# An encoder layer's two branch projections by seven block products, with lasting buffer pools and a pinned order around the feed-forward and the end

## The chip, the cores and the metric

One NeuronCore of a Trainium2 chip. The metric is the device time of one execution in microseconds (us), the median over several.

## The reference, cut to what matters

One layer is applied to two groups of 512 tokens (g = 0, 1) with the same weights; the model width is 1024, so a tensor is 8 column blocks of 128.

```python
h = rmsnorm(x, g_mix); u = h @ w_in            # split into q, k, v, o, gates, c_q, c_kv, ..., gm
y_m = (sigmoid(o) * hm) @ w_mo                 # hm: normalised mLSTM output
y_a = mla_attention(...) @ w_ao                # 8 heads
g_m, g_a = split(sigmoid(gm))
x = x + (g_m * y_m + g_a * y_a) @ w_out
h2 = rmsnorm(x, g_ffn)
x = x + (silu(h2 @ w_gate) * (h2 @ w_up)) @ w_down      # width 2816 = 22 blocks
x = x + sigmoid(x @ w_ple_gate) * (p @ w_ple)
return rmsnorm(x, g_final)
```

All data is float32. The kernel gets its precision from split operands: a tensor is a high part (rounded, on ScalarE) and a low part (the rest, one subtraction on VectorE), and a product is three matmuls: high x high, low x high, high x low.

## The kernel before, in words

Tokens lie along the free dimension (tiles of 128 x 512, 256 KB); a weight block is 128 x 1024 (512 KB) and is loaded, split and used as the stationary operand. A list scheduler that works with a model of the engines' times sets the order on each engine from the data dependencies, the free buffers and the program's order as priority; a few places are tied by hand (`issue_after`). All DMAs are issued by SP, in one queue. Buffers come from pools (`Slots`) that are opened and closed like a stack; a new pool's tile waits until the tiles that lay on its memory have been read.

The order of the program:

- The input projection's parts, the mLSTM by head, then attention by head (`attn_proj`, `attn`, L668-L738). The merge gates' projections (`merge_gate`, list `BULK`) lie between the heads; their results go to DRAM (`tmd`, `tad`), as do the branches' results (`hzd`, `ozd`).
- Projection of the mLSTM branch, L761-L771: `hx` is split (`gsplit`), then per column block c `w_mo` and both groups, 24 matmuls each by `proj1` (L152-L163). The PSUM pool is attention's (tag `mm`), and the operands take buffers that attention's latents leave, so these products may run between attention's. Results go to DRAM (`z1d`).
- Projection of the attention branch, L772-L791: the same with `w_ao`; merge; split into `y`.
- Output projection, L800-L812: per block c `w_out` for both groups, residual, squares for the norm (`SumSq`).
- The norms of both groups (L813, `rstd_bank`, `spread`: root on VectorE, two diagonal tiles, two matmuls that spread it over the partitions), and the embedding product `p @ w_ple`, 16 blocks of 6 matmuls, tied behind the last output projection (L817-L822). Then pools O, H, EV and WP are closed and OP is opened on their memory (L824-L831).
- Feed-forward operands, L931-L947: per k four normalised tiles, split, and four sums of them on POOL for the seven products.
- Feed-forward by `Seven` (L838-L908): a quad is two weight blocks times both groups with the inner dimension halved, a 2 x 2 by 2 x 2 block product, done by seven products P1, P2, P7, P6, P5, Q4, P3 of 4 x 3 = 12 matmuls (9 in the last part of down) that accumulate in PSUM banks b0, b1, b2. It needs sums of weight blocks (POOL, L879-L889) and of operands. The first gate quad is computed plainly with 96 matmuls (`plain`, L855-L869), while the operands come into being. `run` (L910-L920) chains quads, with the next quad's P1, P2, P7 between the present one's P6, P5, Q4, P3; it is called once for gate and up and once per part of down (three parts, L1037), whose operands are loaded back from DRAM (`actd`) and split first.
- The end, L1040-L1133: `x` is split again, `proj2` multiplies by `w_ple_gate`, `embed` applies tanh, the embedding and the residual, `final_norm` (L1077-L1096) scales and writes. Group 0 is done four blocks ahead of group 1; the last two blocks of group 1 go by token halves.

## Time and profile before

| | |
|---|---|
| median of 3 executions | 1949.64 us (1948.28 to 1950.61) |
| the profiled execution's own time | 1949.27 us |
| its span, first to last instruction | 1947.5 us |
| busy: PE / DVE / ACT / POOL | 95% / 59% / 43% / 21% |
| mean granted TensorE clock | 0.978 |

Times in the profile's rows are us from the span's start. PE is TensorE's matmuls, PEld its weight loads, DVE is VectorE, ACT is ScalarE, POOL is GpSimd, SP issues DMAs. A row names the line of the kernel before, the engine, the operation and `out<-in` by the program's tile names. Matmuls overlap each other, so their busy time is longer than the distance from one to the next.

### The profile page before, as it was taken

The numbers are of one execution on the slowest core, as the hardware profiler recorded it, in microseconds if no ns is written. First come the engines' busy times: TensorE is split into PE (matmuls) and PEld (weight loads), VectorE is DVE, ScalarE is ACT, GpSimd is POOL, SyncE is SP. The second block draws the span as 40 slices with busy tenths as digits, with TensorE's granted clock in tenths as the row PEclk, the third lists the DMA queues.
The fourth block names the chain that finished last, engine by engine and source line by source line (L and its number), as shares of the span: only waits on it lengthen the run. The fifth ranks groups of instructions, "written<-read, shape, count | busy, mean of one in ns | idle before, by whom it ended". The sixth has DMA issues, their size and how long they took to land.

```text
span 1947.5 us, 24431 instructions
## 1 busy us (share of the span) xinstructions
PE 1855.9 (95%) x8922; PEld 1554.3 (80%) x8922; DVE 1146.6 (59%) x2021; ACT 830.9 (43%) x1608; POOL 400.5 (21%) x313
## 2 busy tenths in 40 slices
PE   7999999999999999999999948999999989999993
PEld 6889898988888788788888827888888867888883
DVE  7757575746455666854445455444454448967655
ACT  5245454535354566852122234333333335533332
POOL 3000000100000000100001033665566472323002
PEclk9999999999999999999999978999999999999996
DMA  4111111012252212457335110232232337633322
GB/s 160 50 44 33 55 44 55 33 60 82 82 181 87 71 63 82 136 194 227 109 112 191 64 65 27 95 127 92 98 115 102 103 127 246 197 100 99 108 65 87
DMA packets 94424, 198.15 MB, mean 102 GB/s; under 512 B 10272, under 2 KB 20896, under 8 KB 94304
## 3 DMA queue, kind: packets, MB, share of 16 engines
q1 hardware_dynamic: 94304, 196.59, 30.0%
q8 instruction: 70, 1.15, 0.2%
q14 instruction: 50, 0.41, 0.1%
HBM read 142.45 MB, written 54.10 MB: 101 GB/s over the span
## 4 chain that ended last, share of the span: by engine, by line
PE 88%; DVE 6%; ACT 2%; DMA 1%; issue 1%; POOL 1%; SPq 0%; DVEq 0%; ACTq 0%; POOLq 0%
PE mm L160 11%; PE mm L162 11%; PE mm L161 11%; PE b L904 10%; PE b L905 10%; PE b L906 10%; PE nm L548 3%; DVE xl L133 2%; PE mm L465 2%; PE mm L467 2%; PE mm L466 2%; PE mm L1065 1%; PE mm L1066 1%; PE mm L1064 1%; PE pt L726 1%
## 5 line engine op out<-in xcount | busy, mean ns | idle before, releaser
L904 PE MATMUL b<-xh,wh 128*128 128x512 f32 x896 | 346.0, 391 | 13.7 <-ACT xh L137 7.7
L905 PE MATMUL b<-xl,wh 128*128 128x512 f32 x896 | 349.6, 390 | 0.0
L906 PE MATMUL b<-xh,wl 128*128 128x512 f32 x896 | 346.5, 390 | 0.0
L133 DVE TENSOR_TENSOR wl<-wst,wh 128x512 fp32r<-128x512 f32 (+1 forms) x226 | 200.9, 890 | 154.9 <-ACT wh L851 134.0
L851 ACT CAST wh<-wst 128x512 fp32r<-128x512 f32 (+1 forms) x202 | 122.7, 609 | 284.2 <-PE b L905 246.4
L160 PE MATMUL mm<-hh,whi 128*128 128x512 f32 x592 | 233.4, 395 | 7.2 <-ACT whi L147 7.0
L162 PE MATMUL mm<-hh,wlo 128*128 128x512 f32 x592 | 232.6, 395 | 2.3 <-DVE wlo L133 2.2
L161 PE MATMUL mm<-hl,whi 128*128 128x512 f32 x592 | 233.5, 395 | 0.8 <-DVE hl L247 0.8
L904 PEld LDWEIGHTS b<-xh,wh 128*128 128x128 f32 x896 | 168.9, 189 | 50.9 <-ACT xh L137 8.2
L906 PEld LDWEIGHTS b<-xh,wl 128*128 128x128 f32 x896 | 168.9, 188 | 35.3
L905 PEld LDWEIGHTS b<-xl,wh 128*128 128x128 f32 x896 | 168.9, 188 | 35.2 <-DVE xl L133 0.2
L147 ACT CAST whi<-wst 128x1024 fp32r<-128x1024 f32 (+1 forms) x79 | 81.5, 1032 | 142.9 <-PE mm L161 122.6
L160 PEld LDWEIGHTS mm<-hh,whi 128*128 128x128 f32 x592 | 112.5, 190 | 30.8 <-ACT whi L147 7.0
L162 PEld LDWEIGHTS mm<-hh,wlo 128*128 128x128 f32 x592 | 112.4, 190 | 26.2 <-DVE wlo L133 3.4
L161 PEld LDWEIGHTS mm<-hl,whi 128*128 128x128 f32 x592 | 112.2, 189 | 25.2 <-DVE hl L247 1.9
L879 POOL TENSOR_TENSOR s<-wst,wst 128x512 f32<-128x512 f32 (+1 forms) x33 | 44.9, 1359 | 386.4 <-DMA wst<-w 300.4
L133 DVE TENSOR_TENSOR wlo<-wst,whi 128x1024 fp32r<-128x1024 f32 (+1 forms) x79 | 96.5, 1221 | 28.3 <-ACT whi L147 27.6
L133 POOL TENSOR_TENSOR vnl<-avt,vnh 128x512 fp32r<-128x512 f32 x16 | 21.1, 1317 | 357.8 <-ACT vnh L137 217.1
L962 DVE TENSOR_TENSOR u<-b,u 128x512 f32<-128x512 f32 x63 | 43.4, 688 | 71.1 <-PE b L906 71.1
L1014 DVE TENSOR_TENSOR x<-x,b 128x512 f32<-128x512 f32 x84 | 56.9, 681 | 38.1 <-PE b L906 37.9
L465 PE MATMUL mm<-whi,hh 128*128 128x256 f32 x256 | 72.0, 283 | 0.4 <-DVE cu L299 0.4
L466 PE MATMUL mm<-whi,hl 128*128 128x256 f32 x256 | 72.0, 283 | 0.0
(311 smaller groups left out, 3977.4 us busy)
## 6 DMA issues: line engine op xcount, KB each, us to landing
wst<-w SPq DMA_DIRECT2D x125, 512.0 KB
ld<-actd SPq DMA_DIRECT2D x77, 256.0 KB
actd<-t SPq DMA_DIRECT2D x44, 256.0 KB
actd<-sg SPq DMA_DIRECT2D x33, 256.0 KB
x<-x SPq DMA_DIRECT2D x32, 256.0 KB
wst<-wd SPq DMA_DIRECT2D x16, 512.0 KB
hzd<-hz SPq DMA_DIRECT2D x16, 256.0 KB
tmd<-tg SPq DMA_DIRECT2D x16, 256.0 KB
```

What stands on the lines that cost most here:

```text
L133: e.tensor_tensor(out=out, in0=src, in1=hi.bitcast(F32), op=ALU.subtract)
L147: S.copy(hi[:, :n], st[:, :n])
L160: E.matmul(bk, whi[:, c], hi, start=k == 0, stop=False)
L161: E.matmul(bk, whi[:, c], lo, start=False, stop=False)
L162: last_mm[0] = E.matmul(bk, wlo[:, c], hi, start=False, stop=k == nk - 1)
L465: E.matmul(out, hi[:, tb], whi[:, n], start=k == 0, stop=False)
L466: E.matmul(out, lo[:, tb], whi[:, n], start=False, stop=False)
L548: E.matmul(bk, l, r, start=n == 0, stop=n == len(terms) - 1)
L851: S.copy(hi, src)
L904: E.matmul(bk, whi[:, c], hi, start=bool(first) and k == 0, stop=False, **sk)
L905: E.matmul(bk, whi[:, c], lo, start=False, stop=False, **sk)
L906: E.matmul(bk, wlo[:, c], hi, start=False, stop=k == self.kh - 1, **sk)
```

## The change

- `w_mo` and `w_ao`: blocks c and c+4 of a weight form a quad for `Seven`; the eight quads run in one chain (`chain`, in place of `run`), which calls for operands (`need`) four products ahead. The class `Ops` makes a product's operand when it is called for; sums of operands are on VectorE or POOL by a rule of each use. Three of the mLSTM branch's operands are called for before attention's last head. The chain's PSUM banks are opened behind attention.
- Pools H, EV, WP, a new WX and the new OP last to the end; split weights take turns in five buffers of WP and WX. The X2 pool, which later holds `x`, holds the raw operands.
- The output projection does all blocks of group 0 and then all of group 1, so that each `w_out` block is loaded and split twice. Group 0's norm lies inside group 1's products (`mid`).
- The root is spread by four matmuls of its column, broadcast, with the identity (`spread_f32`), in place of two diagonal tiles and two matmuls.
- From the last output projection on the order on PE, ACT, DVE and POOL is the program's (`pinned`); the embedding products are dealt out between the steps of group 1's norm and the first operands.
- All feed-forward quads, gate/up and down, form one chain; the first gate quad goes by seven products too; the chain begins with P1 and P2 of two quads.
- In the end group 0 is six blocks ahead, the order is pinned, group 0's output lies between group 1's blocks, and the token halves of the last two blocks are interleaved.

The diff, cut to its core:

```diff
--- before.py
+++ after.py
+    pinned = [False]
+
+    class Engine:
+
+
+        def __init__(self, e):
+            self.e = e
+
+        def __getattr__(self, name):
+            f = getattr(self.e, name)
+
+            def call(*args, **kw):
+                r = f(*args, **kw)
+                if pinned[0]:
+                    tc.keep_in_program_order(r)
...
-    def proj1(w, x, nk=KD, off=0, bn="mm", tok=slice(0, T)):
+    def proj1(w, x, nk=KD, off=0, bn="mm", tok=slice(0, T), mid=None):
         whi, wlo = w
         bk = bank(bn)[:, tok]
         for k in range(nk):
             c = slice(off + k * P, off + (k + 1) * P)
+            if mid and k == nk - 3:
+                mid()
...
+    def spread_f32(r, b0=0, nb=NB, bn="rbc"):
+        bc = bank(bn)
+        for i in range(nb):
+            E.matmul(
+                bc[:, (b0 + i) * P : (b0 + i + 1) * P], r[:, 2 * i : 2 * i + 1].to_broadcast([P, P]), ident,
+                start=True, stop=True,
+            )
+        return bc[:, b0 * P : (b0 + nb) * P]
...
+    Q = Slots("Q", tr=3, qkv=12, qst=4, p=3, ph=1, pl=1)
     QL = Slots("QL", lat=16)
-    Q = Slots("Q", tr=3, qkv=12, qst=4, p=3, ph=1, pl=1)
...
+    WX = Slots("WX", "right", wst=2, s3=2, wp=1)
...
-        w = w8(f"mo{c}")
-        for g in range(G):
-            t = load(tmd[g][c], QL, "lat")
-            V.scalar_tensor_tensor(out=t, in0=t, scalar=1.0, in1=proj1(w, hx[g]), op0=ALU.add, op1=ALU.mult)
-            nc.sync.dma_start(z1d[g][c], t)
...
-    OP = Slots("OP", op=OPS, ev=8)
...
+    def op(name, n, dt):
+        return (H if name in ("P1", "P2", "P7", "P6") else late["OP"])("h", n, dt)
...
+        def part(self, name, k):
+            if name in ("P1", "P2", "P3"):
+                return self.get({"P1": "a", "P2": "c", "P3": "d"}[name], k)
+            add = self.sums(name).tensor_tensor
+            if name == "P7":
+                t = self.t[k] = self.tmp()
+                add(out=t, in0=self.get("b", k), in1=self.get("d", k), op=ALU.subtract)
+            elif name == "P6":
+                t = self.t[k]
+                add(out=t, in0=t, in1=self.get("a", k), op=ALU.subtract)
+            elif name == "P5":
+                t = self.get("a", k)
+                add(out=t, in0=t, in1=self.get("b", k), op=ALU.subtract)
+            else:
+                t = self.t[k]
+                add(out=t, in0=t, in1=self.get("c", k), op=ALU.add)
+            return t
...
+        sl, tag = ((WP, "whi"), (WP, "wlo"), (WX, "wp"), (WP, "whi"), (WP, "wlo"))[wpn[0] % 5]
+        wpn[0] += 1
+        return sl(tag, "wp", F32R, (P, 1024))
...
-        def plain(self, put):
-
-            ws = [[self.split(self.st[2 * i + j]) for j in range(2)] for i in range(2)]
...
+    def chain(quads, head=False, look=4):
+
+        order = [(0, n) for n in ("P1", "P2", "P7")]
...
+            order = [(0, "P1"), (0, "P2"), (1, "P1"), (1, "P2"), (0, "P7"), (0, "P6"), (0, "P5"), (0, "Q4"), (1, "P7"), (0, "P3")]
...
+            for i, m in order[at : at + look + 1]:
+                quads[i][0].need(m)
+            for i, m in order[at : at + 2]:
+                if i not in made:
+                    made[i] = quads[i][1]()
+            made[q].product(n)
...
+            QL.close()
+            X2 = Slots("X2", "right", x=16)
+            for n in ("P1", "P2", "P7"):
+                hops.need(n)
...
+    late["OP"] = Slots("OP", h=24, sg=4, ev=8)
...
+    banks("PF", dict(b0=2, b1=3, b2=2, sp=1), b0="b0", b1="b1", b2="b2", sp="sp")
...
+            m = load4(tmd[g][cc])
+            V.scalar_tensor_tensor(out=m, in0=m, scalar=1.0, in1=t, op0=ALU.add, op1=ALU.mult)
+            nc.sync.dma_start(z1d[g][cc], m)
...
+            z = load4(z1d[g][cc])
+            y = load(tad[g][cc], late["OP"] if c == 0 else X2, "sg" if c == 0 else "x")
+            V.scalar_tensor_tensor(out=y, in0=y, scalar=1.0, in1=t, op0=ALU.add, op1=ALU.mult)
+            V.tensor_tensor(out=y, in0=y, in1=z, op=ALU.add)
+            yr[g][cc] = y
...
+    oops = Ops(lambda g, k: load(ozd[g][k], X2, "x"), lambda: late["OP"]("ev", "t"), lambda n: V if n == "P7" else GP)
...
+    chain([pair("mo", c, hops, put_z(c)) for c in range(4)] + [pair("ao", c, oops, put_y(c)) for c in range(4)])
...
+        for k in (0, 4, 1, 5, 2, 6, 3, 7):
+            t = yr[g][k]
+            hi = H("h", "yh", F32R)
+            S.activation(out=hi, in_=t, func=AF.Copy, scale=0.5)
+            lo = H("h", "yl", F32R)
+            V.scalar_tensor_tensor(out=lo, in0=t, scalar=0.5, in1=hi.bitcast(F32), op0=ALU.mult, op1=ALU.subtract)
+            y[g][k] = (hi, lo)
...
+    h2 = Ops(hn, lambda: OP("ev", "t"), lambda n: GP if n == "Q4" else V)
...
+    for c in range(KD):
+        out_proj(0, c)
+    pp, wple = [], []
+    for c in range(KD):
+        pinned[0] = c == KD - 1
+        out_proj(1, c, {0: lambda: sums(0), 1: lambda: spread2(0)}.get(c))
+        if c == 0:
+            inv(0)
+        if 2 <= c < 6:
+            h2.need("P1", [c - 2])
+            h2.need("P2", [c - 2])
...
+    emb(2)
+    sums(1)
+    emb(1)
+    inv(1)
+    emb(1)
+    spread2(1)
+    emb(2)
+    for k in range(4):
+        h2.get("b", k)
+        h2.get("d", k)
+        emb(1)
+        h2.need("P7", [k])
+        emb(1)
+    emb(len(todo))
+    pinned[0] = False
+    for n in ("P6", "P3", "P5", "Q4"):
+        h2.need(n)
...
-        if f1 == 0:
-            make("fg", None)().plain(gate)
-            return [make("fu", up)]
...
+    chain(quads, head=True)
...
+    for c in range(LEAD):
+        w = halves(c)
         for g in range(G):
             embed(c, g, proj2(w, x3[g]))
-    for c in range(lead, KD):
-        embed(c, 0, proj2(wpg(c), x3[0]))
-    ws = [wpg(c) for c in range(lead, lead + 2)]
-    final_norm(0)
-    for c in range(lead, KD - 2):
-        bk = proj2(ws.pop(0), x3[1])
-        ws.append(wpg(c + 2))
-        embed(c, 1, bk)
-    last = [load(emd[1][c], OP, "ev") for c in range(KD - 2, KD)]
-    for b0, nb in ((0, NB // 2), (NB // 2, NB // 2)):
-        tok = slice(b0 * P, (b0 + nb) * P)
-        for c in range(KD - 2, KD):
-            embed(c, 1, proj2(ws[c - KD + 2], x3[1], tok), tok, last[c - KD + 2])
-        final_norm(1, b0, nb, (2, 5) if b0 else range(KD))
+    for c in range(LEAD, KD):
+        embed(c, 0, proj2(halves(c), x3[0]))
+    w = halves(LEAD)
+    pinned[0] = True
...
+    bk = [proj2(ws[0], x3[1], toks[0])]
+    embed(*last)
+    finish(0, [4, 5])
+    bk.append(proj2(ws[1], x3[1], toks[0]))
+    embed(KD - 2, 1, bk[0], toks[0], bps[0])
+    finish(0, [6])
+    bk.append(proj2(ws[0], x3[1], toks[1]))
+    embed(KD - 1, 1, bk[1], toks[0], bps[1])
+    finish(0, [7])
+    sums(1, 0, H0)
+    inv(1, H0)
+    bk.append(proj2(ws[1], x3[1], toks[1]))
+    embed(KD - 2, 1, bk[2], toks[1], bps[0])
+    spread3(1, 0, H0)
+    finish(1, [0, 1, 2, 3], 0, H0)
+    embed(KD - 1, 1, bk[3], toks[1], bps[1])
+    sums(1, H0, H0)
+    inv(1, H0)
+    rs_ = rs2[1]
+    spread3(1, H0, H0)
+    rs2[1], rs_ = rs_, rs2[1]
+    finish(1, [4, 5, 6, 7], 0, H0)
+    rs2[1] = rs_
+    finish(1, list(range(KD)), H0, H0)
```

## Rows read from the trace of the kernel before

**Rows 1.** The page: busy time by engine, and PE's share in 40 slices, in tenths.

```profile
PE 1855.9 (95%) x8922; PEld 1554.3 (80%) x8922; DVE 1146.6 (59%) x2021; ACT 830.9 (43%) x1608; POOL 400.5 (21%) x313
...
PE   7999999999999999999999948999999989999993
```

**Rows 2.** One line's instructions, L160: ns min/median/max, first and last start us.

```profile
L160 PE MATMUL mm<-oxh,whi x128: 389/389/389, 936.1 to 1022.5; 128*128 128x512 f32 x128
...
L160 PE MATMUL mm<-yh,whi x128: 389/389/389, 1023.2 to 1109.5; 128*128 128x512 f32 x128
```

**Rows 3.** Stages: length, busy us (instructions) of each engine, granted clock, DMA share, GB/s.

```profile
817.00:872.00 55.00, 55.00 (x269) 45.70 (x268) 37.31 (x78) 38.05 (x73) 2.97 (x2) 1.00 0.64 216
936.00:1023.00 87.00, 87.00 (x386) 72.03 (x385) 40.30 (x54) 17.91 (x23) 0.00 (x0) 1.00 0.33 107
1109.50:1196.30 86.80, 52.59 (x216) 40.66 (x215) 53.97 (x81) 32.95 (x56) 25.75 (x17) 0.78 0.13 49
1130.00:1175.00 45.00, 10.79 (x33) 6.21 (x31) 30.52 (x33) 14.72 (x26) 18.15 (x12) 0.62 0.09 33
1200.00:1580.00 380.00, 380.00 (x1678) 314.64 (x1677) 175.59 (x209) 137.10 (x237) 224.58 (x150) 1.00 0.31 105
1580.00:1627.00 47.00, 35.31 (x147) 27.96 (x145) 28.22 (x42) 23.32 (x41) 17.20 (x13) 0.93 0.60 206
1627.00:1700.00 73.00, 71.87 (x308) 59.00 (x309) 63.26 (x90) 37.20 (x64) 22.50 (x15) 0.98 0.58 195
1700.00:1815.00 115.00, 115.00 (x509) 95.20 (x509) 84.08 (x126) 41.92 (x75) 33.44 (x25) 1.00 0.33 106
```

**Rows 4.** PE's waits: for whom; us in total, times, longest.

```profile
PE b L866 <- ACT xh L137: 33.2, 4, 12.4
```

**Rows 5.** Timeline, ScalarE, then VectorE: start, us, [idle before, releaser].

```profile
1135.14 0.59 ACT L821 COPY em<-mm 128x512 f32<-128x512 f32 x1 [0.77 <-PE mm L162]
1135.63 0.62 ACT L137 CAST xh<-hn 128x512 fp32r<-128x512 f32 x1
...
1136.28 0.69 DVE L133 TENSOR_TENSOR xl<-hn,xh 128x512 fp32r<-128x512 f32 x1 [13.98 <-ACT xh L137]
1136.89 0.74 DVE L935 SCALAR_TENSOR_TENSOR hn<-x,cols,rbc 128x512 f32<-128x512 f32 x1
```

**Rows 6.** Timeline, PE, first products of the plain gate quad.

```profile
1176.21 0.63 PE L866 MATMUL b<-xh,wh 128*128 128x512 f32 x1
1176.64 0.63 PE L867 MATMUL b<-xl,wh 128*128 128x512 f32 x1
```

**Rows 7.** Timeline, PE, where gate/up gives way to down.

```profile
1605.52 1.22 PE L904 MATMUL b<-xh,wh 128*128 128x512 f32 x2 [7.74 <-ACT xh L137]
```

**Rows 8.** Timeline of the end: PE, VectorE, ScalarE, PE.

```profile
1913.01 0.28 PE L1066 MATMUL mm<-xh,wl 128*128 128x256 f32 x1
...
1907.11 6.20 DVE L1092 SCALAR_TENSOR_TENSOR o<-x,cols,rsf 128x512 f32<-128x512 f32 x6 [4.12 <-ACT rsf L1081]
...
1927.28 3.30 ACT L1089 ACTIVATE o<-x,cols 128x256 f32<-128x256 f32 x8
1930.48 0.36 ACT L1107 ACTIVATE pt<-mm 128x256 f32<-128x256 f32 x1
...
1935.76 0.98 PE L198 MATMUL ssc<-onesr,sq 128*128 128x2 f32 x4 [8.78 <-DVE sq L236]
```

**Rows 9.** Stages, instructions on tile mm alone (w_mo's products beside attention).

```profile
817.00:845.00 28.00, 12.16 (x44) 8.12 (x44) 0.00 (x0) 0.00 (x0) 1.00 0.91 308
845.00:872.00 27.00, 16.82 (x70) 12.93 (x71) 2.64 (x4) 0.00 (x0) 1.00 0.36 120
```

**Rows 10.** Groups by line and form: feed-forward (VectorE, POOL), projections 936-1110 (VectorE): busy, mean ns.

```profile
L133 DVE TENSOR_TENSOR wl<-wst,wh 128x512 fp32r<-128x512 f32 x120 | 118.4, 987 | 123.5 <-ACT wh L851 123.5
...
L879 POOL TENSOR_TENSOR s<-wst,wst 128x512 f32<-128x512 f32 x20 | 26.0, 1300 | 101.8 <-DMA wst<-w 101.6
...
L133 DVE TENSOR_TENSOR pll<-ld,plh 128x512 fp32r<-128x512 f32 x4 | 2.7, 690 | 3.5 <-ACT plh L137 3.5
```

More of the change, by code (lines that the diff above doesn't have):

```diff
@@ L833, in split_op, with __init__, get, need @@
-    def split_op(src):
-        return split(src, OP, "op", "x")
+    late = {}
+    NAMES = ("P1", "P2", "P7", "P6", "P5", "Q4", "P3")
+    def op(name, n, dt):
+        return (H if name in ("P1", "P2", "P7", "P6") else late["OP"])("h", n, dt)
+    class Ops:
+        def __init__(self, raw, tmp, sums):
+            self.raw, self.tmp, self.sums = raw, tmp, sums
+            self.r, self.t, self.x = {}, {}, {}
+        def get(self, n, k):
+            if (n, k) not in self.r:
+                self.r[n, k] = self.raw({"a": 0, "b": 1, "c": 0, "d": 1}[n], k + 4 * (n in "cd"))
+            return self.r[n, k]
+        def part(self, name, k):
[15 more added lines that the diff above has]
+            return t
+        def need(self, name, ks=range(4)):
+            x = self.x.setdefault(name, [])
+            for k in ks:
+                if len(x) == k:
+                    src = self.part(name, k)
+                    hi = op(name, "xh", F32R)
+                    S.copy(hi, src)
+                    lo = op(name, "xl", F32R)
+                    lo_of(lo, src, hi)
+                    x.append((hi, lo))
@@ new lines, in encoder_kernel, with __call__, sums, inv @@
+    OP = late["OP"]
+    banks("P3", dict(mm=5, tp=1, bc=2), mm="mm", tp="ssc", bc="rbc")
+    class Sl:
+        def __call__(self, tag, n, dt=F32, shape=(P, T)):
+            return OP("ev" if tag in ("ch", "tr") else "h", n, dt, shape)
+    sl = Sl()
+    x2 = [[None] * KD for _ in range(G)]
+    ss = [SumSq(sl, "tr") for _ in range(G)]
+    pc, r2, rs2 = {}, {}, {}
+    def sums(g, b0=0, nb=NB):
+        pc[g] = bank("ssc")
+        sumsq(pc[g], ss[g].sq, b0, nb)
+    def inv(g, nb=NB):
+        r2[g] = rsqrt(pc[g][:, 0 : 2 * nb], 2 * nb, 1.0 / D)
@@ L1038, in encoder_kernel @@
     f0 = 0
     for pi, nf in enumerate(FF_PARTS):
-        run(down(pi, f0, nf))
+        quads += down(pi, f0, nf // 2)
         f0 += nf
+    chain(quads, head=True)
     banks("P4", dict(mm=5, tp=1, bc=2), mm="mm", tp="ssc", bc="rbc")
-    def halves(src):
-        st = W("wst", "wst", F32, (P, 1024))
-        nc.sync.dma_start(st, src)
-        out = []
-        for j in range(2):
-            hi = W("wh", "wh", F32R)
-            S.copy(hi, st[:, j * T : (j + 1) * T])
-            lo = W("wl", "wl", F32R)
-            lo_of(lo, st[:, j * T : (j + 1) * T], hi)
-            out.append((hi, lo))
-        return out
@@ L1058, in proj2, with halves @@
-    def proj2(ws, x, tok=slice(0, T)):
+    x3 = [[None] * KD for _ in range(G)]
+    for c in range(KD):
+        for g in range(G):
+            x3[g][c] = split(x2[g][c], H, "h", "x")
+    ss = [SumSq(sl, "h") for _ in range(G)]
+    def halves(c):
+        st = (WP, WX)[c % 2]("wst", "wst", F32, (P, 1024))
+        nc.sync.dma_start(st, a["w8"][W8[f"pg{c}"]])
+        return [wsplit(st[:, j * T : (j + 1) * T]) for j in range(2)]
+    def proj2(ws, x, tok=slice(0, T), mid=None):
         bk = bank()[:, tok]
@@ new lines, in encoder_kernel @@
+    ws = [w, halves(KD - 1)]
+    bps = [load(emd[1][c], OP, "ev") for c in range(KD - 2, KD)]
+    toks = [slice(0, T // 2), slice(T // 2, T)]
+    H0 = NB // 2
+    bk = [proj2(ws[0], x3[1], toks[0])]
+    embed(*last)
+    finish(0, [4, 5])
[7 more added lines that the diff above has]
+    inv(1, H0)
```

386 lines of the change are left out of this document (185 added, 201 removed).

## The prediction

> **What bounds the kernel now.** I read the page first. TensorE (PE) is busy 95% of the span and no other engine over 59%; the 40 slices show 9 nearly everywhere, with dips at slices 24-25, at slice 33 and in the last one [rows 1]. So only two things can shorten this kernel: fewer matmul columns, or less time in which PE stands. The price of a matmul is not its 389 ns of busy time, since matmuls overlap: the w_ao projection's 384 matmuls start at 936.1 and w_out's at 1023.2 [rows 2], so one costs 87.1/384 = 0.227 us, and a block product of 12 costs 2.72 us. Then the table by stage [rows 3] gives the holes: 936-1023, 1200-1580 and 1700-1815 are full, 1130-1175 has 10.8 busy of 45.0, 1580-1627 has 35.3 of 47.0, and the end stands largely empty (part 4 below). The waits [rows 4] say who ends the first hole: ScalarE's split of the feed-forward operands, 33.2 us in 4 waits. ScalarE in turn begins those splits at 1135.6, right behind its last copy of the embedding product, although the first normalised operand had been written long before [rows 5]: the operands' pool lies on the memory of the pools that the embedding product still uses. From there VectorE builds operands in a row: 0.74 for one normalised tile, 0.69 for one low part [rows 5].
>
> **1. Seven products instead of eight.** For w_mo and w_ao two column blocks c and c+4 and both groups took 4 x 24 = 96 matmuls; the seven products take 7 x 12 = 84. Eight such quads save 96 matmuls, the first gate quad of the feed-forward (plain before) another 12. 108 x 0.227 = **24.5 us** off, all on PE, which is full there [rows 3].
>
> **2. In front of the feed-forward.** From the last w_out matmul (1109.5) to the first regular product (1196.3) are 86.8 us [rows 3]. Work that stays in it: 96 embedding matmuls and 96 of the plain quad, 192 x 0.227 = 43.5. The other **43.3 us** are holes, and matmuls at the lower of the two clocks (1.2 GHz): granted 0.62 of 2.4 GHz on average in 1130-1175, with 0.43 us between two matmuls still at 1176 [rows 3, 6]. The change makes the pools last, so that operands need not wait for the embedding product; projects group 0 through w_out before group 1 (43.6 us of matmuls under which group 0's norm and eight of its splits fit); and pins the order, so that 16 embedding products (21.8 us) lie over group 1's norm. Is VectorE short enough? Behind group 1's norm it has 8 normalised tiles and 4 differences and low parts for P7, 8 x 0.74 + 8 x 0.69 = 11.4, with some 3 us of waiting for ScalarE, under the 16.3 us of the 12 embedding products that remain. Then P6, P3, P5 and Q4 take 24 x 0.69 = 16.6 us, plus a weight split per product (0.69), while the order of the first quads gives five products, 13.6 us, before P6. It fits nearly; P5 may be late by 2 or 3 us. With the sums and the spreading matmuls of group 1's norm (under 2 us) I leave 5: **38 us** off (bounds: 28, if VectorE's work is late next, to 41).
>
> The eight further weight loads of w_out (each 1 ScalarE cast, 1 VectorE subtraction, 512 KB) cost nothing while 24 matmuls, 5.4 us, cover some 2.3 us of splitting; without cover 8 x 2.3 = 18. SP issues eight more DMAs, in a stretch where it has room.
>
> **3. From gate/up into down.** 11.7 us of holes in 1580-1627, 1.1 behind it, a little lower clock [rows 3]; the longest was 7.7 us for the split of a loaded activation [rows 7]. One chain over both now lets the first down quad's P1 run between the last products of gate/up, with its operands needed four products ahead. The 28 loads stand in the same SP queue as the weights, so 3 us stay: **10 us** off (5 to 12). The changes between parts of down, in 1700-1815, were already free [rows 3].
>
> **4. The end.** From the last matmul (1913.0, 0.28 long) to the end at 1947.5 are 34.2 us [rows 8]. VectorE first does six output tiles of group 0 (6.2 us) that it could have done earlier, and the two token halves follow each other, each with its norm, with ScalarE's eight scalings (3.3) and POOL's products between [rows 8]. Pinned, group 0's output is finished under group 1's matmuls, and the first half's sums stand before the last 24 half-wide matmuls. After the last matmul remain one embedding tile and four outputs on VectorE, about 5 us (two tiles took from 1930.5 to 1935.8 [rows 8]); then the sums, the root, the spread, outputs and the last DMA. That stretch is 11.7 us now (1935.8 to 1947.5); it loses diagonal building and a copy (some 2) and gets four more half tiles (4 x 0.43). So 16.5 us: **18 us** off (13 to 20).
>
> **5. What it costs: the end of attention.** From 817 to 872 w_mo's matmuls filled what attention left: 44 + 70 = 114 matmuls, 25.8 us of 55 [rows 9]. Now the chain's PSUM pool opens only behind attention, over attention's banks, so I count on three products (8.2 us) as filler. ScalarE was busy 38.1 us in that stretch [rows 3] and gets 12 more casts of 0.62 [rows 5] before attention's last head: 45.6. If attention shrinks to that, PE stands 45.6 - 29.2 - 8.2 = 8 us; if it keeps its 55 us, 17.6; if the scheduler finds filler, 0. Nothing of before shows attention without filler behind its last head; I take **8**, since ScalarE's time is the nearest measured limit.
>
> **6. What it costs: sums in the new chain.** POOL, idle in 936-1023 before [rows 3], now adds weights (4 of 1.3 us a quad) and operands (12 a set). VectorE's low part takes 0.69 us alone and 0.99 in the feed-forward stage, where POOL runs [rows 10]. In 672 x 0.227 = 152 us the chain holds some 160 VectorE operations with both inputs in SBUF, 110 us at 0.69, and 32 + 24 = 56 POOL sums of 1.3, 73 us. If the two engines can't overlap at all there, 183 us, less some 27 that are done under attention: 4 to 31 over. If they overlap like in the feed-forward, where PE stayed full, 0. I take **7**, near the lower end, because the feed-forward rows are the nearest case.
> The Trainium skill's page "SBUF — State Buffer", section "Who interferes with whom", says that a VectorE instruction with two SBUF inputs and a GpSimd one that reads SBUF exclude each other for the whole instruction. By that rule alone the term would be the 31 rather than 7. The trace bears out that they slow each other (0.99 against 0.69), but in 1200-1580 PE did not stand for it.
>
> **Sum.** -24.5 - 38 - 10 - 18 + 8 + 7 = -75.5 against a span of 1947.5, which gives 1872; with the 1.8 us around the span (the profiled execution took 1949.3, the median of three is 1949.6) **1874 us**.
>
> **Rivals.**
> - A, forecast, 1862 to 1888: 0.62.
> - B, the projections starve: the junction costs 18 and the chain 31, as in 5 and 6; 1874 + 10 + 24 = 1908, half of it 1891. For it: VectorE must rebuild 28 operands while w_mo gives way to w_ao, 28 x 0.99 = 28 us beside a quad of 19. Against: each operand's buffers come free six products (16 us) ahead. 0.2.
> - C, the hole in front of the feed-forward only halves, because the operands' 39 us on VectorE are what is late: +15, 1889. Against: most now lie under w_out and the embedding. 0.07.
> - D, the change doesn't do what it says: SBUF reuse and the scheduler bring the same holes back, and only part 1 pays: 1949.3 - 24.5 + 15 = 1940. 0.03.
> - E, slower: products separated by waits run PE at the lower clock. It happened at 1130-1175, and there a matmul costs 0.43 instead of 0.227 [rows 3, 6]. All 672 projection matmuls at that rate cost 134 us more, 2008 us; it decides from some 370 of them on. Against: the same chain in 1200-1580 kept a clock of 1.00. 0.03.
> - F, better, with no junction or sum cost: 1859 and below. 0.05.
>
> **The numbers.** About 0.2% (4 us) is what a measurement of this kernel can tell from no change; only D's neighbourhood could come near it. Faster 0.95, same 0.02, slower 0.03. The range takes in A, F, C and B up to nearly its full price: 1854 to 1904.
>
> **What would show it.** Right: 84 matmuls a quad in both projections; no PE wait over 3 us between the last w_out matmul and the first gate product; the last matmul some 16 us before the end; short waits for ScalarE or VectorE around the end of attention. Wrong: a granted clock well under 1.00 or POOL and VectorE both near full in the projections' stretch (B, E); a wait of feed-forward products for the splits (C); ScalarE's first split behind the last embedding copy again (D).

## The result, and the profile after

The changed kernel took **1939.3 us** (median of 4 runs, 1937.5 to 1942.4) beside 1949.3 before (4 runs, 1948.3 to 1950.6): ratio 0.995, 95% interval 0.9933 to 0.9967. It is faster, by 10 us and not by the 75 of the forecast, and it lies above the forecast range. The page of the changed kernel, busy time and PE's slices:

```profile
PE 1861.9 (96%) x8836; PEld 1542.6 (80%) x8836; DVE 1260.3 (65%) x2135; ACT 874.7 (45%) x1711; POOL 474.4 (24%) x349
...
PE   7999999999999999979899989999999999999997
```

The old dips at slices 24-25, at 33 and at the end [rows 1] are shallower, but there are new ones, at slices 18 and 20. Stretches of [rows 3] again (length, busy us of PE, PEld, VectorE, ScalarE and POOL, granted clock, DMA share, GB/s):

```profile
817.00:872.00 55.00, 40.66 (x179) 31.68 (x178) 40.64 (x79) 45.23 (x91) 16.57 (x11) 0.84 0.29 101
936.00:1023.00 87.00, 81.11 (x341) 65.00 (x340) 81.59 (x100) 36.23 (x65) 47.16 (x26) 0.96 0.53 175
1109.50:1196.30 86.80, 75.97 (x305) 59.03 (x304) 64.42 (x89) 40.70 (x71) 26.15 (x17) 0.92 0.25 88
...
1200.00:1580.00 380.00, 373.82 (x1610) 301.78 (x1609) 184.28 (x203) 130.39 (x232) 214.56 (x144) 1.00 0.30 99
1580.00:1627.00 47.00, 45.24 (x190) 36.43 (x189) 38.07 (x46) 23.08 (x42) 25.03 (x16) 0.96 0.61 206
```

Three stretches that were full are no longer: 817-872 (40.7 of 55), 936-1023 (81.1 of 87) and, the least visible, 1200-1580 (373.8 of 380, and 1610 matmuls where 1678 ran before). Read the count there and not only the busy time: matmuls overlap, so short pauses hardly show in busy us, but 68 fewer matmuls at 0.227 us are 15 us lost.

Fixed windows catch different work in the two kernels. So I cut both traces, and those of all experiments, at four events: the start of the first w_out matmul, of the first gate product and of the last matmul of the down products, and the end of the span; all begin at 817. For "before" and the forecast, the 21.8 us of the plain gate quad's matmuls are moved to the third column, where the changed kernel has that quad. The forecast's columns follow from its terms (for the first, 206.2 - 21.8 + 8 + 7).

| kernel | 817 to w_out | w_out, embedding | feed-forward | end | median us | ratio to before, 95% |
|---|---|---|---|---|---|---|
| before | 206.2 | 151.4 | 649.2 | 123.6 | 1949.3 | |
| forecast | 199.4 | 113.4 | 636.5 | 105.6 | 1874 | |
| changed | 219.4 | 129.8 | 664.1 | 107.7 | 1939.3 | 0.9933-0.9967 |
| e1_swap | 220.4 | 130.5 | 651.1 | 107.4 | 1928.6 | 0.9875-0.9901 |
| e17_after_ring41 | 219.9 | 129.2 | 653.7 | 107.6 | 1927.5 | 0.9873-0.9906 |
| e6_unpinned | 220.4 | 113.0 | 664.9 | 108.9 | 1925.5 | 0.9859-0.9889 |
| e18_after_entry | 219.8 | 113.0 | 664.2 | 107.3 | 1922.8 | 0.9854-0.9884 |
| e4_early | 219.9 | 123.9 | 659.1 | 107.6 | 1932.0 | 0.9892-0.9917 |
| e3_fill | 214.2 | 131.4 | 665.5 | 107.7 | 1935.8 | 0.9906-0.9942 |
| e5_vsums | 215.0 | 133.5 | 662.3 | 108.0 | 1937.6 | 0.9924-0.9949 |
| e7_all | 210.6 | 123.1 | 650.8 | 108.0 | 1909.8 | 0.9783-0.9810 |
| e8_nopin | 211.2 | 113.0 | 657.4 | 109.2 | 1909.3 | 0.9784-0.9811 |
| e9_endpin | 211.3 | 112.9 | 658.1 | 108.0 | 1907.7 | 0.9774-0.9800 |
| e10_nopin_early | 211.1 | 113.0 | 656.8 | 109.2 | 1908.7 | 0.9780-0.9807 |
| e14_ring4 | 213.8 | 113.7 | 656.5 | 108.8 | 1910.3 | 0.9782-0.9810 |
| e15_ring4and1 | 210.6 | 113.0 | 648.0 | 108.9 | 1899.8 | 0.9726-0.9753 |
| e16_fill2 | 210.2 | 112.9 | 659.2 | 109.4 | 1909.1 | 0.9773-0.9800 |

Against the forecast the changed kernel lost 20.0 us in front of w_out, 16.4 at the entry of the feed-forward, 27.6 in the feed-forward and 2.1 at the end: 66 us. The last is small. The other three were told apart by experiments; none of them leaves out any of the computation.

### The profile page after: what moved, and what is told of

It reads as the page before. It is cut to its first block, busy times and chain, and to the rows that moved or that the text cites. A ratio compares the mean times of both kernels' runs of the same rounds, so it can differ in the third digit from the quotient of the medians.

```text
span 1938.0 us, 24531 instructions
## 1 busy us (share of the span) xinstructions
PE 1861.9 (96%) x8836; PEld 1542.6 (80%) x8836; DVE 1260.3 (65%) x2135; ACT 874.7 (45%) x1711; POOL 474.4 (24%) x349
## 5 line engine op out<-in xcount | busy, mean ns | idle before, releaser
L77 PE MATMUL b<-xh,wp 128*128 128x512 f32 x2296 | 723.4, 396 | 17.9 <-ACT wp L77 8.3
L77 PEld LDWEIGHTS b<-xh,wp 128*128 128x128 f32 x2296 | 434.5, 190 | 124.4 <-ACT wp L77 11.7
L77 PE MATMUL b<-xl,wp 128*128 128x512 f32 x1148 | 452.4, 394 | 5.9 <-DVE xl L77 5.7
L77 DVE TENSOR_TENSOR wp<-wst,wp 128x512 fp32r<-128x512 f32 (+1 forms) x284 | 271.9, 964 | 108.8 <-ACT wp L77 108.0
L77 ACT CAST wp<-wst 128x512 fp32r<-128x512 f32 (+1 forms) x284 | 171.0, 611 | 345.4 <-PE b L77 228.1
L77 PEld LDWEIGHTS b<-xl,wp 128*128 128x128 f32 x1148 | 217.8, 190 | 54.3 <-DVE xl L77 7.6
L77 POOL TENSOR_TENSOR wst<-wst 128x512 f32<-128x512 f32 (+1 forms) x84 | 125.7, 1496 | 35.3 <-DVE wp L77 30.7
L77 DVE TENSOR_TENSOR u<-b,u 128x512 f32<-128x512 f32 x90 | 61.3, 687 | 107.6 <-PE b L77 82.7
L77 DVE TENSOR_TENSOR xl<-ld,xh 128x512 fp32r<-128x512 f32 x109 | 88.7, 846 | 8.1 <-ACT xh L77 7.8
L77 PE MATMUL mm<-xh,wp 128*128 128x512 f32 (+1 forms) x288 | 81.7, 368 | 0.0
L77 ACT COPY u<-b 128x512 f32<-128x512 f32 x90 | 50.9, 586 | 66.6 <-PE b L77 65.6
```

The source lines that it names most:

```text
L77: r = f(*args, **kw)
```

## The experiments

### Feed-forward: in which order do buffers come free?

The gate and up products, full before, now wait for ScalarE or VectorE, and ScalarE itself waits differently. ScalarE's waits in 1230-1560 (for whom: us in total, times, longest), before and then after:

```profile
ACT wh L851 <- PE b L905: 166.0, 98, 3.0
```

```profile
ACT wp L77 <- PE b L77: 131.0, 44, 5.4
ACT wp L77 <- DMA wst<-w: 53.9, 11, 8.3
```

Before, ScalarE paced itself product by product: 98 short waits for a split's buffer. After, it waits for a split's buffer half as often, up to 5.4 us, and 53.9 us more for weight loads. ScalarE's timeline of the changed kernel shows the pattern (start, us, ... [idle before, releaser]):

```profile
1292.50 0.62 ACT L77 CAST wp<-wst 128x512 fp32r<-128x512 f32 x1 [1.62 <-PE b L77]
1298.48 0.62 ACT L77 CAST wp<-wst 128x512 fp32r<-128x512 f32 x1 [5.36 <-PE b L77]
1300.30 0.62 ACT L77 CAST wp<-wst 128x512 fp32r<-128x512 f32 x1 [1.19 <-PE b L77]
1303.06 0.62 ACT L77 CAST wp<-s 128x512 fp32r<-128x512 f32 x1 [2.14 <-PE b L77]
1303.59 0.62 ACT L77 CAST wp<-wst 128x512 fp32r<-128x512 f32 x1
...
1310.59 1.14 ACT L77 CAST wp<-wst 128x512 fp32r<-128x512 f32 x2 [5.42 <-DMA wst<-w]
```

Splits come in bursts in place of one per 2.72 us product, and the copies and activations behind a late one on ScalarE come late too. Two edits of buffers were candidates. First, the two load blocks, f1 and f2, of a set of seven products: f1's always took its buffer from WP (free when P3 is split), f2's from WX (free already at Q4), while before both drew on four common ones. As each pool has two such buffers, the edit lets the blocks trade pools after every two sets:

```diff
+            qn[0] += 1
-            for sl, src in zip((WP, WX), srcs):
+            for sl, src in zip((WP, WX) if qn[0] // 2 % 2 == 0 else (WX, WP), srcs):
```

> The changed kernel, but the two weight blocks of a set of seven products trade pools every second set, so that the block that the next set needs first (f1) always takes the buffer that came free first (at Q4's split, not at P3's). Theory 'late block': the changed kernel loses some 20 us in the steady gate and up products (it lost 0 before) because f1's load waits for the later of two buffers; then feed-forward takes 644 to 655 us in place of 664, ScalarE no longer waits tens of us for weight loads between 1230 and 1560, and the time falls from 1939 to 1920 to 1930. Rival 'chained engines' (the loss comes from ScalarE and VectorE being fuller or in another order, whatever buffer is used): feed-forward stays within 4 us of 664 and the time within 4 us of 1939.

Measured 1928.6, feed-forward 651.1: as the theory said, and of ScalarE's 53.9 us of waits for loads 0.9 are left, though 651 is still 15 over the forecast. The reverse, in the kernel before:

```diff
-    W = Slots("W", "right", wst=4, s3=2, wh=5, wl=5)
+    W = Slots("W", "right", wst=2, wsu=2, s3=2, wh=5, wl=5)
...
-            for src in srcs:
-                t = W("wst", "wst", F32, (P, 1024))
+            for tag, src in zip(("wst", "wsu"), srcs):
+                t = W(tag, "wst", F32, (P, 1024))
```

> The kernel before, with its four common weight buffers cut into two fixed pairs, f1's blocks always in one and f2's in the other, as the changed kernel has them; nothing else. Theory 'late block': the gate and up products, full before, lose 12 to 20 us, waits for weight loads appear on ScalarE, and the time rises from 1949 to 1960 to 1970. Rival 'chained engines': within 3 us of 1949.

**A miss:** 1948.7 (ratio 0.9984 to 1.0001). Fixed load buffers do no harm by themselves, so the theory lacked its other half. That half was the second edit of buffers, which I had read over in the diff: high and low part of a split share one tile, and these tiles come from three tags with 2, 2 and 1 buffers in a fixed rotation, where there had been five and five from one tag each. Put into the kernel before, with the fixed load buffers and then without:

```diff
-    W = Slots("W", "right", wst=4, s3=2, wh=5, wl=5)
+    W = Slots("W", "right", wst=2, wsu=2, s3=2, wa=2, wb=2, wc=1)
...
+        return W(("wa", "wb", "wc", "wa", "wb")[(wpn[0] - 1) % 5], "wp", F32R, (P, 1024))
```

> The kernel before with its weights handled as in the changed one: fixed pairs of load buffers for f1 and f2, and high and low part of a split in one tile out of three rings of 2, 2 and 1 in fixed rotation, in place of five and five from one ring each. The fixed pairs alone gave 1948.7. Theory 'pairs and rings together': feed-forward, 627.7 us before, rises by 10 to 16 us and the time to 1958 to 1966, with waits for weight loads of tens of us on ScalarE between 1230 and 1560. Rival 'operand side' (the loss of the changed kernel comes from its other tiles: the results u and sg out of five small pools, the order in which they are made): within 3 us of 1949.

> The kernel before with the three rings for the split weights alone, its four load buffers common as they were. With rings and fixed load buffers together it took 1960.4, with fixed load buffers alone 1948.7. Theory 'both together': neither alone costs more than 3 us, since the rings only hurt when the load comes late: 1947 to 1952. Rival 'the rings alone': 1957 to 1963.

With both 1960.4 (1.0048 to 1.0073), with the rings alone 1957.0 (1.0022 to 1.0050). So the rings (one for each tag) hurt alone, by 7 us, at the low end of that rival's range; with fixed load buffers, harmless alone, it is 11, though the two intervals just touch. ScalarE's waits of the first of these two runs in 1230-1560 repeat the picture of the changed kernel; with the rings alone, below, the waits for loads are missing and the long ones for buffers stay:

```profile
ACT wp L858 <- PE b L912: 121.5, 43, 5.3
ACT wp L858 <- DMA wst<-w: 51.9, 13, 6.7
```

```profile
ACT wp L858 <- PE b L912: 163.5, 69, 5.4
...
ACT wp L858 <- DMA wst<-w: 0.7, 1, 0.7
```

Is it the rings, or that two parts share a tile? One ring of five such tiles in the kernel before (wa=5, every split from "wa"):

> The kernel before with high and low part of each weight split in one tile out of a single ring of five, its load buffers common as they were. With three rings of 2, 2 and 1 in place of the one it took 1957.0 beside 1950.4. Theory 'rings': one ring of five pairs is as good as five and five, 1948 to 1952. Rival 'pair tile' (high and low part come free together, only with the last product that reads either): 1955 to 1959, as with three rings.

1948.0 (0.9981 to 0.9999): the shared tile is free, the division into rings costs. A reason can be read in the order of ScalarE's instructions. In the kernel before, and with one ring, none of the 235 splits of the feed-forward stands behind one that the code makes later. With three rings 68 of the 235 of e13 and 77 of the 294 of the changed kernel (its projections' included) stand right behind one that the code makes later: the planner, the list scheduler, can take a split whose own ring has a buffer free ahead of one that waits for another ring, and the product that was in need first waits. That this overtaking is what costs the time is argued, not shown: e1 has 81 such places and still took 13 us off the stage, and with three rings a split also has to wait for its own ring's buffer while another ring has one free, whether or not it is overtaken. So give the changed kernel a larger ring:

```diff
-    WP = Slots("WP", wst=2, whi=2, wlo=2)
+    WP = Slots("WP", wst=2, w=4)
...
-        sl, tag = ((WP, "whi"), (WP, "wlo"), (WX, "wp"), (WP, "whi"), (WP, "wlo"))[wpn[0] % 5]
+        sl, tag = ((WP, "w"), (WP, "w"), (WX, "wp"), (WP, "w"), (WP, "w"))[wpn[0] % 5]
```

> The changed kernel with one edit, the split weights out of two rings, one of four pairs and one of one, in place of three of 2, 2 and 1. Theory 'rings': feed-forward falls from 664 by 10 to 18 us, since the late load of f1 also matters less then, and the time from 1939 to 1920 to 1929. Rival 'late load' (fixed load buffers are what is left to hurt): 1934 or more.

1927.5, feed-forward 653.7 (10.4 less), 32 such places in place of 77. The gate and up stretch is full again, with 13 matmuls fewer than before, and ScalarE's waits for loads fall to a third:

```profile
1200.00:1580.00 380.00, 380.00 (x1665) 312.11 (x1664) 179.93 (x206) 133.45 (x235) 218.21 (x148) 1.00 0.30 103
```

```profile
ACT wp L77 <- PE b L77: 114.1, 48, 5.3
ACT u L77 <- PE b L77: 57.5, 33, 4.2
ACT wp L77 <- DMA wst<-w: 18.7, 5, 5.0
```

### The entry: what does the written order do?

Timeline of PE, 1130 to 1167, waits of the changed kernel:

```profile
1138.14 0.50 PE L77 MATMUL mm<-plh,wp 128*128 128x512 f32 x1 [0.30 <-ACT wp L77]
1145.38 0.50 PE L77 MATMUL mm<-plh,wp 128*128 128x512 f32 x1 [1.24 <-ACT wp L77]
1147.27 1.22 PE L77 MATMUL mm<-plh,wp 128*128 128x512 f32 x2 [1.16 <-DVE wp L77]
1156.36 0.50 PE L77 MATMUL mm<-plh,wp 128*128 128x512 f32 x1 [2.28 <-ACT wp L77]
```

The embedding waits for the splits of its own weights, which the written order puts right in front of their use, behind operand work on ScalarE and VectorE. I first moved only these splits:

```diff
-            if c // 2 == len(wple):
+            while len(wple) <= min(3, c // 2 + 1):
...
+        w = w8(f"out{c}")
         pinned[0] = c == KD - 1
```

> The changed kernel, but each of the four splits of the embedding's weights is made one block of four products earlier, and the last split of the output projection's weights is taken out of the written order. Theory 'just in time': embedding and feed-forward's entry lose 14 us of which 8 to 9 are waits for the splits that stand right in front of their use; the stage falls from 36 to 27 to 30 us, the last products of the output projection win 2 more, and the time falls to 1928 to 1933. Rival 'clock and h2': the stage is bounded by the normalised operands of feed-forward and the holes move behind the embedding; the time stays within 3 us of 1939.

1932.0, inside the theory's range, but the stage gained only 5.9 us. The waits for the embedding's splits are gone, and a new one stands behind the embedding, much as the rival had it: PE waits 10.5 us for ScalarE's last copies of the embedding out of its PSUM banks, which the written order keeps behind a cast that itself waits for VectorE's operand. PE, then ScalarE of this run:

```profile
1160.85 0.80 PE L77 MATMUL b<-xh,wp 128*128 128x512 f32 x1 [10.46 <-ACT em L77]
...
1153.20 0.62 ACT L77 CAST xh<-t 128x512 fp32r<-128x512 f32 x1 [5.34 <-DVE t L77]
...
1159.73 1.55 ACT L77 COPY em<-mm 128x512 f32<-128x512 f32 x3
```

Then the written order was switched off at both places, and later at the entry alone:

```diff
-                if pinned[0]:
+                if False:
```

> The changed kernel with its written order switched off, in front of feed-forward and at the end; all the rest as it is. It shows what the pins are worth by themselves. Theory 'pins pay at the end, not at the entry': the tail after the last matmul of the down products goes back from 107 to 117 to 123 us, the entry stays 33 to 39 us: time 1947 to 1957. Rival 'pins pay at both': entry over 50 us and time over 1960. Rival 'pins pay nowhere': within 4 us of 1939, and the gains at both places came from the seven products' pools and the other moves.

```diff
-        pinned[0] = c == KD - 1
+        pinned[0] = False
```

> The changed kernel with one edit, the written order off in front of feed-forward and kept at the end. With it off at both places the time was 1925.5. Theory 'the entry's order costs, the end's is worth 1 to 3 us': 1922 to 1926. Rival: the end's order gave something that the entry's took, 1918 or less, or the gain came from the end, 1934 or more.

1925.5 and 1922.8. **My three theories of the first were all wrong**, since all let the order help or be idle at the entry; it costs 16.5 us there (1939.3 to 1922.8), and the stage falls from 129.8 to 113.0, which is the forecast's 113.4. Of these 16.8 us PE stood 9.2, 6.3 for the embedding's splits and 2.9 for the last split of w_out; the rest goes with the clock, granted 0.95 on average over the stage and 1.00 without the order. The stretch of the embedding, changed kernel and then without the entry's order:

```profile
1130.00:1166.00 36.00, 29.73 (x114) 22.60 (x114) 26.63 (x45) 18.71 (x34) 10.12 (x7) 0.86 0.36 132
```

```profile
1122.00:1151.00 29.00, 29.00 (x136) 24.11 (x135) 13.79 (x27) 14.05 (x27) 10.83 (x8) 1.00 0.52 180
```

Both hold all but a few matmuls of the embedding, the one with 6 us in which PE stands and a granted clock of 0.86, the other full and at 1.00. The groups of the second stretch on PE say what fills it:

```profile
L77 PE MATMUL mm<-plh,wp 128*128 128x512 f32 x61 | 19.4, 395 | 0.0
L77 PE MATMUL mm<-pll,wp 128*128 128x512 f32 x31 | 12.1, 391 | 0.0
L77 PE MATMUL mm<-yh,wlo 128*128 128x512 f32 x8 | 3.1, 392 | 0.0
L77 PE MATMUL mm<-yh,whi 128*128 128x512 f32 x7 | 2.7, 392 | 0.0
L77 PE MATMUL mm<-yl,whi 128*128 128x512 f32 x7 | 2.7, 389 | 0.0
```

The planner keeps the last 22 matmuls of w_out (mm from yh and yl) back and lays them between the embedding's. The written order forbids just that.

### In front of w_out: attention's end and the shared port

The chain's first product starts with attention's last matmul. One tile's instructions (x, ns min/median/max, first and last start), and PE's waits in 817-1037:

```profile
L77 PE MATMUL b<-xh,wp x84: 389/389/400, 871.4 to 899.9; 128*128 128x512 f32 x84
```

```profile
PE sc L77 <- ACT p L77: 8.5, 3, 3.6
PE b L77 <- DVE xl L77: 5.7, 3, 5.3
PE pt L77 <- DVE apl L77: 2.5, 2, 1.4
PE av L77 <- DVE apl L77: 2.1, 1, 2.1
```

So the filler of three products doesn't exist: not one lies under attention. Two merge gates of 24 matmuls were put behind attention's last head, taken from the middle of attention:

```diff
-            for n in ("P1", "P2", "P7"):
-                hops.need(n)
+            for k in range(4):
+                for n in "acbd":
+                    hops.get(n, k)
...
-BULK = [10, 2, 1, 1, 0, 2, 0, 0, 0, 0]
+BULK = [10, 2, 1, 1, 0, 0, 0, 0, 0, 2]
```

> The changed kernel, but two of the merge gates' 24-matmul steps stand behind attention's last head in place of in front of it, and the operands of the first three products are made behind them, their raw loads and scalings in front. Theory 'no filler': the 22 us that the changed kernel loses between 817 and the first products come from TensorE having only attention left while ScalarE sets its pace; with products to issue behind it the junction loses 5 to 10 us and the time falls to 1922 to 1932. Rival 'engines full': ScalarE and VectorE owe the same work anyway, the first product only waits later for its operands, and the time stays within 4 us of 1939; if the operands come too late it is up to 8 us slower.

1935.8: the stage gains 5.2 us, at the small end of the first theory, but the time is above that theory's 1922 to 1932 and within the second's 4 us, and its interval overlaps the changed kernel's: it doesn't decide. The other hole of this stage is VectorE's. VectorE and POOL beside each other in the changed kernel:

```profile
952.65 1.78 DVE L77 SCALAR_TENSOR_TENSOR ld<-ld,u 128x512 f32<-128x512 f32 x1
953.84 1.75 POOL L77 TENSOR_TENSOR ld<-ld,ld 128x512 f32<-128x512 f32 x1
954.36 1.78 DVE L77 TENSOR_TENSOR xl<-t,xh 128x512 fp32r<-128x512 f32 x1
955.55 1.74 POOL L77 TENSOR_TENSOR t<-t,ld 128x512 f32<-128x512 f32 x1
956.06 1.78 DVE L77 SCALAR_TENSOR_TENSOR ld<-ld,u 128x512 f32<-128x512 f32 x1
957.26 1.74 POOL L77 TENSOR_TENSOR ld<-ld,ld 128x512 f32<-128x512 f32 x1
...
967.34 1.73 POOL L77 TENSOR_TENSOR wst<-wst 128x512 f32<-128x512 f32 x1
967.86 0.67 DVE L77 SCALAR_TENSOR_TENSOR ld<-ld,b 128x512 f32<-128x512 f32 x1
```

The starts alternate, 1.71 us for one of each: no overlap gained. VectorE's operations that read one input from PSUM (`b`), as at 967.86, keep their 0.67. With all operand sums on VectorE:

```diff
-    hops = Ops(hraw, lambda: (lambda s: s[0](s[1], "t"))(tmps.pop(0)), lambda n: V if n == "P7" else GP)
+    hops = Ops(hraw, lambda: (lambda s: s[0](s[1], "t"))(tmps.pop(0)), lambda n: V)
```

> The changed kernel, but in both branch projections the sums of operands run all on VectorE in place of six of seven on GpSimd. Theory 'shared port': in 950 to 970 VectorE's operations with two operands in SBUF take turns with GpSimd's (1.75 us each against 0.6 alone) and TensorE waits 5 us for them; alone on VectorE a sum and its split take some 1.3 us in place of 3.5, and the hole of 5 us closes: time 1932 to 1936. Rival 'VectorE is the bound': VectorE is already 20.0 of 20 us busy there, six more sums on it push the low parts back further: 1941 to 1950.

1937.6 (1.7 less, the two intervals overlap), between the two theories' ranges. The stage fell by 4.4 us, and 3.7 were given back at the entry. VectorE now does the same operations one behind the other:

```profile
955.02 0.68 DVE L77 TENSOR_TENSOR xl<-t,xh 128x512 fp32r<-128x512 f32 x1
955.62 0.68 DVE L77 TENSOR_TENSOR t<-t,ld 128x512 f32<-128x512 f32 x1
956.23 0.68 DVE L77 TENSOR_TENSOR xl<-ld,xh 128x512 fp32r<-128x512 f32 x1
```

A sum and a split take 1.2 us on VectorE alone, where one operation on each engine took 1.71.

### Together

> The changed kernel with all four edits together: weight pools that trade places, two merge gates behind attention, earlier splits of the embedding's and the last output weights, operand sums on VectorE. Theory 'separate losses': the gains of the four add up, 10.8 for the pools, 7.3 for the splits, 3.5 for the filler and what the sums bring by themselves (0 to 6): time 1912 to 1920. Rival 'one chain of engines' (each edit only shifts the same backlog of ScalarE and VectorE to the next stage): the time stays at or above 1926, no better than the best single edit by more than 3 us.

1909.8: the losses were separate ones. The best single edit of these four had given 1928.6, and the four gains added up would give 1916. Without the written order in place of the early splits:

> The changed kernel with the pools that trade places, the two merge gates behind attention and the operand sums on VectorE, and the written order switched off everywhere. Theory 'the written order at the entry queues late work in front of ready work': the 13.7 us that switching it off gave by itself come on top of 10.8, 3.5 and 1.7 of the three other edits, time 1907 to 1913. Rival 'same backlog': the entry's gain and the pools' overlap, time 1916 or more. If it comes under 1905 the edits help each other.

> The kernel of the run above, but with the written order kept at the end (the last products and the tail) and off only in front of feed-forward. The changed kernel's end took 107.7 us from the last down product to the end of the span with the order written out and 108.9 with it off. Theory 'the end's order is worth little by itself, the split halves are what shortens it': within 3 us of the run above, at most 2 faster. Rival 'the end's order matters': 5 us or more faster than the run above.

> The kernel of the run before last (no written order, pools trading places, merge gates behind attention, sums on VectorE) with the embedding's weight splits one block earlier as well. Theory 'same hole': without a written order the planner already draws these splits forward, so the 7.3 us of the earlier splits fall away: within 3 us of that run. Rival 'separate': 4 us or more faster.

1909.3, 1907.7 and 1908.7: the order at the end is worth 1.2 us by the last column (1.6 between e6 and e18), with overlapping intervals, and the early splits nothing once the planner is free. In e7 PE still stands 10.1 us in front of the feed-forward for ScalarE's copies of the embedding. e8 starts it earlier (113.0 against 123.1) and loses 6.6 of those 10 us there: its first products wait 5.3 us, 3.0 of them for VectorE's weight splits and 1.3 for an operand. On e8's base the last questions, one ring of four pairs, the rings of four and one, and filler from where PE was full (BULK begins with 8 in place of 10, and has its fourth head's two back):

> The version without a written order (pools trading places, two merge gates behind attention, sums on VectorE; 1909.3), with the split weights out of one single ring of four pairs in place of three rings with five. Theory 'rings': although there is one pair less, feed-forward falls from 657 to 645 to 652 and the time to 1898 to 1905. Rival 'number of pairs': four are fewer than five, feed-forward rises and the time is 1912 or more.

> The same version with two rings, one of four pairs and one of one, the fifth split always out of the small one. Theory 'rings' (the more of the pairs share one ring, the better): 1900 to 1907. Rival 'number of pairs': five are five, within 3 us of 1909.

> The same version (1909.3), but the two merge gates behind attention's last head are taken from the ten in front of attention, where TensorE was 60.0 of 60 us busy, and not from attention's fourth head. Theory 'no filler': attention keeps its filler and 5 to 11 us more come back in front of the first products: 1898 to 1904. Rival 'engines full': ScalarE's and VectorE's backlog at attention's end is the same, the time stays within 3 us of 1909.

1910.3, **1899.8** and 1909.1. Four pairs in one ring, where no split overtakes another, are no better than five in three, between both theories' ranges: what the order gives and what the missing pair takes can't be told apart there. Four and one beat both kernels by far (0.9726 to 0.9753), as the theory of the rings had it. More filler from outside attention changed nothing, as the rival had it, but the trace gives another reason than full engines. The merge gates' matmuls (tile mm) of that last run, in the two halves of the stretch, beside [rows 9]:

```profile
817.00:845.00 28.00, 15.37 (x62) 11.39 (x62) 2.06 (x3) 0.00 (x0) 1.00 0.57 207
845.00:872.00 27.00, 0.00 (x0) 0.00 (x0) 0.00 (x0) 0.00 (x0) 0.81 0.39 122
```

Though they stand behind attention's last head in the code, the planner had spent them all by 845, and the last 27 us had none, where there were 70 before.

## Why the prediction was wrong

- **Part 1 (seven products) was right.** Both projections run 8 x 84 = 672 matmuls; without the saving the first stage would be 21.8 us longer still.
- **Part 2 (in front of the feed-forward): right without the written order, wrong with it.** That the change "pins the order, so that 16 embedding products (21.8 us) lie over group 1's norm" counted the order as the carrier of the gain. The gain is there without it, so it comes from what else was changed there (the lasting pools and the projection group by group, which weren't parted); the order itself costs 16.5 us. The wait that I had feared (operands for P6 and P5) isn't what PE stood for; it stood for the embedding's own weight splits, which the forecast doesn't price at all, and for the last of w_out's, costed at nothing because 24 matmuls cover one split. In a written order the split stands behind whatever the code puts in front of it on ScalarE and VectorE, and the cover is gone; with the splits early, ScalarE's copies of the embedding stood there in their place (e4). The sign that I had named, no PE wait over 3 us behind w_out, was met (the longest is 2.3): several short waits and the lower clock behind them made up the loss.
- **Part 3 (gate/up into down) rested on an unsaid premise, and that failed.** Its 10 us were taken from a feed-forward that otherwise stays as it is; 1200-1580 had been full, so I priced nothing there. The change also re-cut the pools of the weight loads and splits, and I costed that at nothing without naming what it rests on: that a buffer which comes free goes to the next in need. The stage came out 27.6 us over the forecast. Of these e17 gave back 10.4; with e15's edits it is 648.0, 11.5 over. The term itself came to half: over the two quads on either side of the change from gate and up to down, PE took 16.4 us more than 0.227 us a matmul in the kernel before, 11.6 in the changed one and 4.0 with e15's edits.
- **Part 4 (the end) was right**: 15.9 us off where 18 were forecast, inside its bounds. The stretch behind the last matmul gave 19.1, and some 3 of them were lost in front of it. PE's last matmul, the last sums and VectorE's last outputs:

```profile
1922.64 0.28 PE L77 MATMUL mm<-xh,wp 128*128 128x256 f32 x1
...
1927.05 0.98 PE L77 MATMUL ssc<-onesr,sq 128*128 128x2 f32 x4 [3.69 <-DVE sq L77]
...
1929.94 4.78 DVE L77 SCALAR_TENSOR_TENSOR o<-x,cols,rbc 128x256 f32<-128x256 f32 x12
```

  From 1922.9 to 1938.0 are 15.1 us where I had 16.5 and before had 34.2. The reason given was half wrong: "pinned, group 0's output is finished under group 1's matmuls" happens unpinned too, for 1 to 2 us more (e6, e9).
- **Part 5 (attention's end) took the wrong end of its range.** The three products as filler were none; ScalarE needed the 45.2 us that I had estimated (45.6), but attention didn't shrink to them: it is a chain between ScalarE, VectorE and PE, and the first product started at 871.4. The stage paid some 22 us (54.4 less the some 32 of attention's matmuls: 206.2 before, less 768 at 0.227), where I took 8 with 17.6 as the bound. My 29.2 for these matmuls ended at 872; before, attention's last one started at 877.9.
- **Part 6 (sums in the chain)**: 871.4 to 1036.4 is 165.0 against 152.4 of matmuls, so 13 where I took 7, inside 4 to 31. The mechanism is the one that I set aside, full exclusion; in the feed-forward, my nearest case, VectorE was 46% busy [rows 3] and had room to wait, in this chain 94% (81.6 of 87). Of the 13, 6 went with the sums on VectorE (165.0 to 159.0 us in e5); the other 7 weren't parted. The Trainium skill's page "SBUF — State Buffer", section "Who interferes with whom", states that a VectorE instruction with two SBUF inputs contends with a GpSimd one that reads SBUF, and that contention for the pair of ports that they share is an exclusive lock. The trace agrees, 0.68 us alone and 1.78 beside POOL.

Rival B (the projections starve) named the first stage rightly, and some 20 of its 34 us were lost there, but it alone would have given 1908 at most. Rival D's time of 1940 was met, but not by its mechanism: the old holes shrank, and the time went in stretches that had none, and at the entry by the order. The late operands of rival C were seen only once the entry's order was gone, and then for some 1.3 us, and E's low clock only for short stretches (0.84 in 817-872, 0.86 in 1130-1166).

**What stays open:** of the 26 us between the best version and the forecast, 11 lie in front of w_out, 12 in the feed-forward and 3 at the end. Filler that is held back until attention's last 27 us wasn't tried. That the rings cost is shown by e12, e13 and e17; that they act through the order of the splits is only argued, since a written order of the splits alone, with three rings, wasn't tried.

## What to carry to other kernels

A change of pools can be a change of order: with a planner that takes what is ready, one ring of five buffers kept the order of the code here, and the same five in three rings let later work overtake and cost 7 us, so price a re-cut of buffers even in a stage that it doesn't name. A written order has to hold also what feeds it: before pinning a stretch, look for each weight split, load and copy out of PSUM in it and where it now stands in its engine's queue, and run the stretch once without the pin. A stage without idle time in the profile isn't safe for that: nothing there hides a new wait.

## What the runs showed of the hardware

A VectorE operation on 128x512 with both inputs in SBUF takes 0.68 us alone and 1.74 to 1.79 beside a POOL sum, whose own record is 1.71 to 1.75; one of each takes 1.71 us in steady alternation, so moving a sum to POOL beside a busy VectorE bought nothing. VectorE's operations that read one input from PSUM and one from SBUF stayed at 0.67 in the same stretch. And PE's granted clock, 1.00 at 2.4 GHz and 0.50 at 1.2 GHz, averaged 0.86 over a stretch with only some 6 of 36 us of waiting (matmuls behind the waits at 1145 and 1147 start 0.43 us apart, in place of 0.23); it was 1.00 throughout when nearly the same products ran without the waits.
